# Layer 1's last two heads attended tile by tile in turns, with their projections placed ahead of them and the output weights loaded earlier

## Chip, cores and metric

The kernel runs on one NeuronCore of one Trainium2 chip. The metric is the device time of one execution in microseconds; for the kernel before it is the median of three runs.

## What is computed

The reference is a two-layer transformer block over 512 latent tokens and 256 context tokens of width 1024, batch 1, all in fp32. Each layer normalises its input and applies a shift and a scale from a conditioning vector, mixes the tokens by attention, adds the gated result, and adds a gated SwiGLU feed-forward part. The change touches layer 1 (the odd one) and the seam to its feed-forward part:

```python
def _diff_attend(q, k, v, lam):
    scale = HEAD_DIM ** -0.5
    def one_block(qb):
        s = jnp.einsum('bqhad,bkhad->bhaqk', qb, k).astype(jnp.float32) * scale
        p = jax.nn.softmax(s, axis=-1)
        a = (p[:, :, 0] - lam * p[:, :, 1]).astype(v.dtype)
        return jnp.einsum('bhqk,bkhe->bqhe', a, v)
...
def finish(o):
    o = _rms(o, subln_w) * (1.0 - lam_init)
    return o.reshape(o.shape[0], o.shape[1], -1) @ w_out
...
x = x + gx1 * ax
x = x + gx2 * _swiglu(_rms(x, norm_ffn_w[l]) * (1.0 + scx2) + shx2, ffn_w_in[l], ffn_w_out[l])
```

Layer 1 has 8 heads. Each head has two score matrices per query token over all 768 tokens (latent and context), and its output is the first softmax less lambda times the second, times the values. In the last layer only the 512 latent tokens are queries.

## The kernel before

All matrices are fp32. For the large products each operand is split into a high part (fp32r, names ending in h or hi) and the rest (names ending in l or lo), and three matmuls per block stand for one product. Tokens are worked on in tiles of 128: tiles 0 to 3 are latent, 4 and 5 context. The kernel is written in Tile: the program order of each engine's queue is dealt by a list scheduler (L1135) from the order of the Python code, priorities and buffers; each engine then works through its own queue in order.

Layer 1's mixer has three strands.

- **Projection.** `in_proj1` (L582) loads and splits a head's weights (SP loads wir, ACT casts wih, POOL or DVE subtracts wil), then for each of six token tiles sums q, k and v (names inps, 24 matmuls of 384 columns for latent tiles, 256 for context tiles, L411 to L413), copies the sum out of PSUM (qkv, ACT, L619), rotates and normalises it (qy on DVE and POOL, L622), splits it (qd and kd, on ACT, DVE L628 and POOL L631), and transposes it two tiles later (qpt L640 to qt L642, kpt L646 to kT L647). The generator `stream` (L1028) yields after each tile; `emit(n)` runs it until n of the 48 tiles are issued.
- **Attention.** One step is one head h and one query tile t, written (h, t). `attend1` computes the scores sc (L662, L663: two halves of four matmuls), their maxima mx (DVE, L665), the exponentials e (ACT, L667), and the difference (DVE, L674); after its yield come the transposes ppt (L681), their copies PT (DVE L684, ACT L686), the product av (L689), and the scaling and norm of the head's output o (L691 to L696). `Staggered.push` (L857) issues a step's first half, then the second half of the step before.
- **Way out.** `out_units` (L699) loads the eight weight rows wo (raw tiles wor, ACT cast woh, subtraction wol on POOL and DVE in turns, L316). `OutProj.operand` transposes a tile's eight head outputs (opt, L726 to L728) and `sums` makes two sums of 24 matmuls (ops, L736 to L738), to which `residual` (L418, L419) applies the gate g and adds x. `norm_hT` then norms the tile for the feed-forward part (square L282, scaling L284, transposes npt L289, hT L295 to L300), and `ffn` (L742) starts with gate and up products (pg, pu, L769) over two segments of 256 tokens, tiles 0 and 1, then tiles 2 and 3.

The loop at L1047 goes over heads, and inside over tiles. Each step is followed by `emit((h + 1) * NT + 2 + (2, 3, 5, 6)[t])`, one or two projection tiles. All 48 are issued by step (6, 2). At (7, 0) the projection's pools close, the weights of way out are asked for, into two shared raw buffers and one of their own, and at (7, 1) to (7, 3) operand and sums of the tile before are issued, the sums at low priority. After the loop come tile 3's operand and sums, four norms and the feed-forward part.

Of the kernel before, what the change touches and what calls it, by code (L numbers as in the profile page):

```python
# [10 lines left out]
F32 = mybir.dt.float32  # L11
F32R = mybir.dt.float32r
# [4 lines left out]
AP = bass.AP  # L17
# [46 lines left out]
def backbone(es: ExitStack, tc: tile.TileContext, x, c, ctx, c_ctx, mod_w, mod_b, norm_mix_w, norm_ffn_w,  # L64
# [179 lines left out]
    def gate_row(l, part, i, pool):  # L244

        if (l, part, i) not in gmem:
            gate_mem(l, part, i)
        g = pool.tile([P, D], F32, name=f"g{i}", tag=f"g{i}")
# [333 lines left out]
    def in_proj1(h, tabs, wp, st, wh, qp, late):  # L582
# [26 lines left out]
        for t in CTX_FIRST:  # L609
# [9 lines left out]
            nc.scalar.copy(raw[:, :n], ps)  # L619
# [15 lines left out]
            def transposes(t=t, nq=nq, qd=qd if nq else None, kd=kd):  # L635
                if nq:
                    pt = tr_tile("qpt", [P, 2, 2, P], F32R)
                    for j in range(2):
                        for a in range(2):
                            nc.tensor.transpose(pt[:, j, a, :], qd[:, j, a].rearrange("p a d -> p (a d)"), identr)  # L640
                    qt = qp.tile([P, 2, 2, P], F32R, name="qt", tag="qt", bufs=5)
                    nc.scalar.copy(qt, f32(pt))  # L642
# [10 lines left out]
    def attend1(h, t, state, o_t, nlam, subln, mp):  # L653
# [53 lines left out]
    class OutProj:  # L707
# [21 lines left out]

        def sums(self, t, bank=None, pool=None, add=nc.vector):  # L730
            ohi, olo = tile_T(0, t), tile_T(1, t)
            for n in range(2):
                ps = acc_tile("ops", one=bank)
                for k in range(KT):
# [3 lines left out]
                    nc.tensor.matmul(ps, olo[:, k, :], a, start=False, stop=k == KT - 1)  # L738
                residual(self.xs[t], ps, self.g[0 if t < NTX else 1], n, pool, add, 1)

# [305 lines left out]
    xs = [None] * NTX  # L1046
    for h in range(8):  # L1047
        for t in range(NTX):
            att.push(attend1(h, t, state[h], o_t, nlam, subln, at.pool))
            if h == 7 and t == 0:  # L1050
                wt.close()
                whi.close()
                wp.close()
                wlo.close()
                states[2].close()
                states[1].close()
                wp = Pool("w1", "right")
                opa = Pool("opa")
# [81 lines left out]
```

## Time and profile before

| | |
|---|---|
| median of 3 runs | 1811.46 us (1810.96 to 1811.88) |
| the profiled execution | 1812.21 us |
| its span, first to last instruction | 1810.4 us |
| mean granted TensorE clock | 0.990 |
| TensorE busy | 1737.3 us, 96% |
| layer 1's projections and attention | about 1030 to 1335 us of the span |
| from the last projection to the feed-forward part | about 1335 to 1424 us |

PE is TensorE's matmuls, PEld its weight loads, DVE VectorE, ACT ScalarE, POOL GpSimd, SP the engine that issues the transfers. In a wait row stand the waiting engine, its output and line, what it waited for, then the total, the number and the longest of the waits. In a row of the timeline stand the start in us from the span's begin, the duration, the engine, the line, the operation, output and inputs, the shape, and in brackets the idle time ahead with its releaser. A matmul's duration includes its way through the array, so that consecutive matmuls overlap: the rate is read from the starts.

### The profile page before, as it was taken

The page shows a single profiled execution, that of the slowest core. Times are in us where ns is not written, and L with a number is a line of the kernel's source. Part 1 is how long each engine was busy: PE and PEld are TensorE (multiplying, and loading weights), DVE is VectorE, ACT ScalarE, POOL GpSimd, SP SyncE. Part 2 cuts the span into 40 slices and gives each one's busy share as a digit, 9 for nine tenths or more (in the row PEclk, how much of TensorE's full clock was granted, in tenths as well). Part 3 has the DMA queues.
Part 4 walks back from the last instruction along what each step waited for, and adds up shares of the span by engine and source line. Part 5 has one row for each costly group of instructions (what it writes and reads, how often), then busy time and mean ns, then how long its engine had stood idle before and what let it go on. Part 6 is the DMA issues. An engine that isn't in the chain of part 4 may idle for free. (4 is left out here: it accounts for less than half of the span.)

```text
span 1810.4 us, 26150 instructions
## 1 busy us (share of the span) xinstructions
PE 1737.3 (96%) x9958; PEld 1456.4 (80%) x9958; DVE 1005.2 (56%) x1703; ACT 823.3 (45%) x1726; POOL 646.9 (36%) x840
## 2 busy tenths in 40 slices
PE   6999999999999999999999989999998999999998
PEld 4887776677888888888888788999986888888886
DVE  4766555444265555555543566666674455655652
ACT  6556556544354444343332656666564532221220
POOL 2864545532064344232210485667633200000000
PEclk9999999999999999999999999999999999999999
DMA  9112222313443234334320321111102332232321
GB/s 322 43 43 86 91 94 82 105 36 121 147 152 117 93 102 143 117 117 140 117 85 1 103 59 54 36 45 45 33 35 93 105 94 93 93 104 83 93 93 47
DMA packets 152477, 165.64 MB, mean 91 GB/s; under 512 B 16480, under 2 KB 139936, under 8 KB 152352
## 3 DMA queue, kind: packets, MB, share of 16 engines
q1 hardware_dynamic: 152000, 163.77, 28.2%
q8 instruction: 78, 1.28, 0.3%
q14 instruction: 47, 0.39, 0.1%
q10 hardware_dynamic: 352, 0.21, 0.0%
HBM read 159.73 MB, written 4.22 MB: 91 GB/s over the span
## 5 line engine op out<-in xcount | busy, mean ns | idle before, releaser
L769 PE MATMUL pg<-hT,wgh 128*128 128x512 f32 (+1 forms) x736 | 244.5, 386 | 3.9 <-ACT hT L299 3.7
L769 PE MATMUL pu<-hT,wuh 128*128 128x512 f32 (+1 forms) x736 | 243.2, 384 | 0.0
L418 DVE TENSOR_TENSOR dps<-dps,g 128x512 f32<-128x512 f32 x200 | 136.0, 697 | 135.0 <-PE dps L823 131.3
L821 PE MATMUL dps<-wdh,hdh 128*128 128x512 f32 x440 | 176.5, 402 | 5.6 <-DVE x L419 3.5
L822 PE MATMUL dps<-wdl,hdh 128*128 128x512 f32 x440 | 174.0, 396 | 0.0
L823 PE MATMUL dps<-wdh,hdl 128*128 128x512 f32 x440 | 166.6, 396 | 0.0
L769 PEld LDWEIGHTS pg<-hT,wgh 128*128 128x128 f32 x736 | 137.0, 189 | 34.4 <-ACT hT L299 3.9
L769 PEld LDWEIGHTS pu<-hT,wuh 128*128 128x128 f32 x736 | 136.6, 189 | 28.6
L769 PE MATMUL pg<-hT,wgl 128*128 128x512 f32 (+1 forms) x368 | 142.0, 386 | 0.0
L769 PE MATMUL pu<-hT,wul 128*128 128x512 f32 (+1 forms) x368 | 141.4, 384 | 0.0
L419 DVE TENSOR_TENSOR x<-x,dps 128x512 f32<-128x512 f32 x200 | 133.5, 684 | 3.4
L411 PE MATMUL inps<-wih,hT 128*128 128x384 f32 x384 | 133.4, 348 | 1.2 <-ACT qkv L619 0.5
L413 PE MATMUL inps<-wih,hT 128*128 128x384 f32 x384 | 131.2, 342 | 0.0
L412 PE MATMUL inps<-wil,hT 128*128 128x384 f32 x384 | 130.8, 341 | 0.0
L197 ACT ACTIVATE modw<-modw,cols 128x256 f32<-128x256 f32 x192 | 82.3, 498 | 69.2 <-DMA modw<-in_mod_w_dram 62.4
L821 PEld LDWEIGHTS dps<-wdh,hdh 128*128 128x128 f32 x440 | 82.7, 188 | 27.9 <-DVE x L419 4.4
L316 DVE TENSOR_TENSOR wul<-wur,wuh 128x1024 fp32r<-128x1024 f32 x44 | 54.9, 1247 | 88.0 <-ACT wuh L315 87.8
L769 PE MATMUL pg<-hTc,wgh 128*128 128x256 f32 x352 | 99.8, 287 | 3.9 <-ACT hTc L299 3.9
L769 PE MATMUL pu<-hTc,wuh 128*128 128x256 f32 x352 | 99.5, 286 | 0.0
L823 PEld LDWEIGHTS dps<-wdh,hdl 128*128 128x128 f32 x440 | 82.7, 188 | 20.2 <-issue 0.4
L796 DVE TENSOR_TENSOR pu<-sg,pu 128x768 f32<-128x768 f32 (+1 forms) x44 | 36.5, 829 | 111.2 <-PE pu L769 97.4
L822 PEld LDWEIGHTS dps<-wdl,hdh 128*128 128x128 f32 x440 | 82.8, 188 | 17.5
(235 smaller groups left out, 4290.6 us busy)
## 6 DMA issues: line engine op xcount, KB each, us to landing
modw<-in_mod_w_dram SPq DMA_DIRECT2D x96, 512.0 KB, 3.9
wgr<-in_ffn_w_in_dram SPq DMA_DIRECT2D x44, 512.0 KB, 3.4
wur<-in_ffn_w_in_dram SPq DMA_DIRECT2D x44, 512.0 KB, 3.4
wdr<-in_ffn_w_out_dram SPq DMA_DIRECT2D x44, 512.0 KB, 3.5
wir<-in_od_w_in_dram SPq DMA_DIRECT2D x96, 128.0 KB, 2.3
x<-in_x_dram SPq DMA_DIRECT2D x8, 512.0 KB, 3.7
wir<-in_ev_w_in_dram SPq DMA_DIRECT2D x16, 256.0 KB, 2.8
wor<-in_ev_w_out_dram SPq DMA_DIRECT2D x8, 512.0 KB, 3.5
```

The lines of the kernel that those rows point to most:

```text
L197: nc.scalar.activation(pr[:, k], w[:, k], AF.Copy, scale=cols[:, kk:kk + 1])
L316: (sub or nc.vector).tensor_sub(lo, raw, f32(hi))
L411: nc.tensor.matmul(ps, hs[0][:, k, :], a, start=k == 0, stop=False)
L412: nc.tensor.matmul(ps, hs[0][:, k, :], b, start=False, stop=False)
L413: nc.tensor.matmul(ps, hs[1][:, k, :], a, start=False, stop=k == KT - 1)
L418: nc.vector.tensor_mul(tmp, ps, g[:, n * 512:(n + 1) * 512])
L419: eng.tensor_add(xt[:, n * 512:(n + 1) * 512], xt[:, n * 512:(n + 1) * 512], tmp)
L769: nc.tensor.matmul(ps[:, s0:s1], a, cols_T(b, s0, s1)[:, k, :], start=k == 0 and q == 0, stop=k == KT - 1 and q == 2)
L796: nc.vector.tensor_mul(pu, sg, pu)
L821: nc.tensor.matmul(ps, hh, a, start=j == 0, stop=False)
L822: nc.tensor.matmul(ps, hh, b, start=False, stop=False)
L823: nc.tensor.matmul(ps, hl, a, start=False, stop=j == nj - 1)
```

## The change

The loop now goes over a list of 32 steps: heads 0 to 5 as before, each over its four tiles, then for each tile head 6 and head 7 in turn: (6, 0), (7, 0), (6, 1), (7, 1) and so on. While i is under 24 each step emits up to `10 + 38 * i // 23` projection tiles, so that all 48 are issued by the end of head 5. At i = 24, ahead of the last eight steps, the projection's pools close and way out's weights are asked for, into the two shared raw buffers alone. The gate row and the residual's scratch get a place in the buffer that context tokens had (`ctx_room`), and the two norm rows another; operand and sums of a tile follow after head 7 of the next tile has begun, and the norms of tiles 0 and 1 are now issued inside the loop, at t = 2 and 3, where head 7 stands. Four buffer counts differ: qkv 4 to 3, qt 5 to 8, o1 2 to 1, and `residual` gets its scratch tiles from outside.

```diff
-            raw = wp.tile([P, 384], F32, name="qkv", tag="qkv", bufs=4)
+            raw = wp.tile([P, 384], F32, name="qkv", tag="qkv", bufs=3)
...
-                    qt = qp.tile([P, 2, 2, P], F32R, name="qt", tag="qt", bufs=5)
+                    qt = qp.tile([P, 2, 2, P], F32R, name="qt", tag="qt", bufs=8)
...
-        o1 = mp.tile([P, P], F32, name="o1", tag="o1", bufs=2)
+        o1 = mp.tile([P, P], F32, name="o1", tag="o1", bufs=1)
...
-    def residual(xt, ps, g, n, pool=None, eng=nc.vector, rb=2):
+    def residual(xt, ps, g, n, tmps=None, eng=nc.vector):
 
-        tmp = ps if pool is None else pool.tile([P, 512], F32, name="rtmp", tag="rtmp", bufs=rb)
+        tmp = ps if tmps is None else tmps[n]
...
-    for h in range(8):
-        for t in range(NTX):
-            att.push(attend1(h, t, state[h], o_t, nlam, subln, at.pool))
-            if h == 7 and t == 0:
...
-                ws = out_units(wp.pool, od_w_out, (nc.gpsimd, nc.vector), (raw_tile, raw_tile, lambda shape, name:
-                               opa.pool.tile(shape, F32, name=name, tag="wor", bufs=1)))
-                oproj = OutProj(1, ws, o_t, xs, opa.pool)
-            if h == 7 and 0 < t <= 3:
-                oproj.operand(t - 1)
-
-                with tc.high_priority(-1000):
-                    oproj.sums(t - 1, 0, opa.pool, nc.gpsimd)
-            emit((h + 1) * NT + 2 + (2, 3, 5, 6)[t])
+    steps = [(h, t) for h in range(6) for t in range(NTX)] + [(h, t) for t in range(NTX) for h in (6, 7)]
+    for i, (h, t) in enumerate(steps):
+        att.push(attend1(h, t, state[h], o_t, nlam, subln, at.pool))
+        if i < 24:
+            emit(10 + 38 * i // 23)
+        if i == 24:
+            for pool in (wt, whi, wp, wlo, states[2]):
+                pool.close()
+            wp = Pool("w1", "right")
+            ws = out_units(wp.pool, od_w_out, (nc.gpsimd, nc.vector))
+            misc, room = ctx_room([P, 2, KT, P], F32, "room")
+            misc = misc.rearrange("p a k q -> p a (k q)")
+            room = [room[:, j] for j in range(2)]
+            oproj = OutProj(1, ws, o_t, xs, misc[:, 0])
+            tmp = [misc[:, 1, 512 * n:512 * (n + 1)] for n in range(2)]
+        if i > 26 and h == 7:
+            oproj.operand(t - 1)
+
+            with tc.high_priority(-1000):
+                oproj.sums(t - 1, 0, tmp, nc.gpsimd)
+            if t > 1:
+                norm_hT(t - 2, xs[t - 2], 1, 1, None, room=room)
     att.flush()
-    for t in range(3, NTX):
-        oproj.operand(t)
-        oproj.sums(t)
-    room = ctx_room([P, 2, KT, P], F32, "nroom")
-    for t in range(NTX):
-        norm_hT(t, xs[t], 1, 1, None, room=[z[:, t % 2] for z in room])
-    opa.close()
+    oproj.operand(3)
+    oproj.sums(3)
+    for t in range(2, NTX):
+        norm_hT(t, xs[t], 1, 1, None, room=room)
+    states[1].close()
```

The scheduler deals the queues anew. The first place is PE's queue at the start of layer 1, where head 0's first latent tiles are transposed (qpt, kpt). Before, the rows that end the projection of a latent tile (its last two are the first two rows here, of 24) stand right ahead of them:

```order
L412 MATMUL inps<-wil,hT_110 128x384
L413 MATMUL inps<-wih,hT_111 128x384
L640 MATMUL qpt<-identr,qd 128x128 x4
L646 MATMUL kpt<-identr,kd 128x128 x2
L640 MATMUL qpt<-identr,qd 128x128 x2
L662 MATMUL sc<-kT,qt 128x256
L663 MATMUL sc<-kT,qt 128x256
L662 MATMUL sc<-kT,qt 128x256
L663 MATMUL sc<-kT,qt 128x256
L640 MATMUL qpt<-identr,qd 128x128 x2
L646 MATMUL kpt<-identr,kd 128x128 x2
```

After, the two last rows of the second context tile's projection (256 columns) stand ahead of them:

```order
L412 MATMUL inps<-wil,hTc_4638 128x256
L413 MATMUL inps<-wih,hTc_4639 128x256
L640 MATMUL qpt<-identr,qd 128x128 x4
L662 MATMUL sc<-kT,qt 128x256
L663 MATMUL sc<-kT,qt 128x256
L662 MATMUL sc<-kT,qt 128x256
L663 MATMUL sc<-kT,qt 128x256
L646 MATMUL kpt<-identr,kd 128x128 x2
L640 MATMUL qpt<-identr,qd 128x128 x4
L646 MATMUL kpt<-identr,kd 128x128 x2
L411 MATMUL inps<-wih,hT_110 128x384
```

The 24 rows of that latent tile's projection have moved behind the transposes of two tiles and the first four scores. On ACT the copy L619 of the second context tile has moved behind both tiles' casts.

The second place is PE's queue at the last projection of all. Before:

```order
L411 MATMUL inps<-wih,hT_110 128x384
L412 MATMUL inps<-wil,hT_110 128x384
L413 MATMUL inps<-wih,hT_111 128x384
L662 MATMUL sc<-kT,qt 128x512
L663 MATMUL sc<-kT,qt 128x512
L662 MATMUL sc<-kT,qt 128x256
L663 MATMUL sc<-kT,qt 128x256
L662 MATMUL sc<-kT,qt 128x512
L663 MATMUL sc<-kT,qt 128x512
L689 MATMUL av<-vv,PT 128x128 x4
L640 MATMUL qpt<-identr,qd 128x128 x4
```

After:

```order
L411 MATMUL inps<-wih,hT_110 128x384
L412 MATMUL inps<-wil,hT_110 128x384
L413 MATMUL inps<-wih,hT_111 128x384
L640 MATMUL qpt<-identr,qd 128x128 x4
L646 MATMUL kpt<-identr,kd 128x128 x2
L662 MATMUL sc<-kT,qt 128x256
L663 MATMUL sc<-kT,qt 128x256
L662 MATMUL sc<-kT,qt 128x256
L663 MATMUL sc<-kT,qt 128x256
L640 MATMUL qpt<-identr,qd 128x128 x4
L646 MATMUL kpt<-identr,kd 128x128 x2
```

Counted over the whole queue, 218 score matmuls of layer 1 (27.25 steps of eight) and 150 products av stand ahead of the last projection matmul before, 200 (25 steps) and 138 after. Behind it, 34 scores stand ahead of the first out-projection matmul before and 36 after. On PE, 91 matmuls of the feed-forward part's first segment stand between tile 3's last ops and its norm's transposes npt before, 67 after. After, the first ops come behind all eight opt of tile 0; before, behind seven.

The third place is SP's and ACT's queue at way out and at the last norm. SP before:

```order
L311 DMA wor<-in_od_w_out_dram 128x1024 x8
L250 DMA g_14081<-gmem 128x1024
L322 DMA x_14377<-out_dram 128x1024
L311 DMA wgr<-in_ffn_w_in_dram 128x4x256 x2
L322 DMA x_14476<-out_dram 128x1024
L311 DMA wur<-in_ffn_w_in_dram 128x4x256 x2
L311 DMA wdr<-in_ffn_w_out_dram 128x1024 x2
```

SP after (the first x is that of tile 2):

```order
L311 DMA wor<-in_od_w_out_dram 128x1024 x6
L322 DMA x_14398<-out_dram 128x1024
L311 DMA wor<-in_od_w_out_dram 128x1024 x2
L250 DMA room_13877<-gmem 128x1024
L311 DMA wgr<-in_ffn_w_in_dram 128x4x256 x2
L322 DMA x_14523<-out_dram 128x1024
L311 DMA wur<-in_ffn_w_in_dram 128x4x256 x2
```

The load of x for tile 2, into the place that o of tile 0 leaves, now stands ahead of the last two rows of way out's weights. ACT before, around the square (L282) and the scaling (L284) of tile 3, x_14476:

```order
L295 ACTIVATE nroom_14547<-npt,modc_107,aff_109 128x128 x4
L282 ACTIVATE nroom_14546,nss<-x_14476 128x1024
L299 CAST hT_110<-nroom_14547 128x4x128
L315 CAST wdh<-wdr 128x1024
L284 ACTIVATE nroom_14546<-x_14476,rs_n 128x1024
L315 CAST wdh<-wdr 128x1024
L315 CAST wgh<-wgr 128x1024
L295 ACTIVATE nroom_14547<-npt,modc_107,aff_109 128x128 x4
```

ACT after, with tile 3 as x_14523:

```order
L295 ACTIVATE room_13878<-npt,modc_107,aff_109 128x128 x4
L299 CAST hT_110<-room_13878 128x4x128
L315 CAST wdh<-wdr 128x1024 x2
L282 ACTIVATE room_13878,nss<-x_14523 128x1024
L315 CAST wgh<-wgr 128x1024
L284 ACTIVATE room_13878<-x_14523,rs_n 128x1024
L315 CAST wgh<-wgr 128x1024
L295 ACTIVATE room_13878<-npt,modc_107,aff_109 128x128 x4
```

Both casts of wd now stand ahead of tile 3's square; before, one stood ahead of the scaling and one behind it.

More of the change, by code (lines that the diff above doesn't have):

```diff
@@ L247, in gate_row @@
             gate_mem(l, part, i)
-        g = pool.tile([P, D], F32, name=f"g{i}", tag=f"g{i}")
+        g = pool if isinstance(pool, AP) else pool.tile([P, D], F32, name=f"g{i}", tag=f"g{i}")
         with tc.issue_after(turn["load"].ins):
@@ L728, in operand, with sums @@
                 nc.vector.tensor_sub(olo[:, 4 * q:4 * q + 4], pt, f32(ohi[:, 4 * q:4 * q + 4]))
-        def sums(self, t, bank=None, pool=None, add=nc.vector):
+        def sums(self, t, bank=None, tmps=None, add=nc.vector):
             ohi, olo = tile_T(0, t), tile_T(1, t)
@@ L738, in sums @@
                     nc.tensor.matmul(ps, olo[:, k, :], a, start=False, stop=k == KT - 1)
-                residual(self.xs[t], ps, self.g[0 if t < NTX else 1], n, pool, add, 1)
+                residual(self.xs[t], ps, self.g[0 if t < NTX else 1], n, tmps, add)
     def ffn(l, xs, ntok, wp, fp, done, mods=()):
@@ L1046, in backbone @@
     xs = [None] * NTX
-    for h in range(8):
-        for t in range(NTX):
-            att.push(attend1(h, t, state[h], o_t, nlam, subln, at.pool))
-            if h == 7 and t == 0:
[L1051 to L1058, printed above, removed]
-                ws = out_units(wp.pool, od_w_out, (nc.gpsimd, nc.vector), (raw_tile, raw_tile, lambda shape, name:
-                               opa.pool.tile(shape, F32, name=name, tag="wor", bufs=1)))
-                oproj = OutProj(1, ws, o_t, xs, opa.pool)
-            if h == 7 and 0 < t <= 3:
-                oproj.operand(t - 1)
-                with tc.high_priority(-1000):
-                    oproj.sums(t - 1, 0, opa.pool, nc.gpsimd)
-            emit((h + 1) * NT + 2 + (2, 3, 5, 6)[t])
```

## Prediction

> **What bounds the kernel now.** The head of the page comes first, with the totals by engine.
>
> ```profile
> span 1810.4 us, 26150 instructions
> PE 1737.3 (96%) x9958; PEld 1456.4 (80%) x9958; DVE 1005.2 (56%) x1703; ACT 823.3 (45%) x1726; POOL 646.9 (36%) x840
> ```
>
> TensorE (PE) works 96% of the span, and the change takes no matmul away. Time can come or go only as idle time or slow clock of PE, so each part below is counted in lost PE time. The windows from layer 1's first projections to its output projection show where it is lost: behind the two times stand the busy us of PE, PEld, DVE, ACT, POOL, then the granted clock.
>
> ```profile
> 1040.00:1060.00 20.00, 17.42 (x119) 16.66 (x118) 8.43 (x17) 9.65 (x24) 18.33 (x26) 1.00 0.28 79
> ...
> 1080.00:1100.00 20.00, 16.85 (x125) 15.62 (x126) 16.80 (x28) 14.14 (x37) 15.14 (x24) 1.00 0.39 113
> ...
> 1120.00:1140.00 20.00, 16.97 (x117) 15.38 (x116) 17.48 (x27) 12.69 (x33) 15.26 (x21) 0.94 0.29 80
> ...
> 1160.00:1335.00 175.00, 171.90 (x1185) 164.03 (x1184) 122.35 (x228) 110.78 (x290) 113.04 (x178) 0.99 0.13 36
> 1335.00:1345.00 10.00, 7.74 (x46) 6.24 (x46) 6.02 (x12) 7.94 (x19) 4.25 (x8) 0.86 0.00 0
> 1345.00:1365.00 20.00, 15.35 (x99) 12.60 (x98) 19.75 (x27) 15.81 (x35) 9.77 (x9) 0.98 0.30 106
> 1365.00:1375.00 10.00, 8.71 (x38) 6.85 (x39) 6.32 (x8) 4.05 (x7) 2.84 (x2) 0.66 0.74 263
> ```
>
> The projection stage is nearly dense (171.90 of 175 us), with losses of about 3 us in three windows early on. The loss comes after it: from 1335 to 1365 PE is busy 23.09 of 30 us while VectorE (DVE) is at 19.75 of 20. PE's waits from 1334 to 1460 name the stalls (total, times, longest).
>
> ```profile
> PE pg L769 <- ACT hT L299: 3.7, 1, 3.7
> PE ops L737 <- DVE wol L316: 3.1, 1, 3.1
> PE sc L662 <- ACT e L667: 1.6, 3, 0.8
> ...
> PE ppt L681 <- DVE hT L728: 1.2, 1, 1.2
> ...
> PE kpt L646 <- POOL kd L631: 0.8, 1, 0.8
> ```
>
> 3.7 us are lost before the feed-forward part's second segment (tile 3's norm), 3.1 us on a way out's weight that DVE had not split, 1.2 us on a transposed attention output right after.
>
> Slow clock comes on top. PE's rows show it (start, us), from the first score behind the last projection at 1334.82 to the first out-projection matmuls at 1357.45 and those 15 us later:
>
> ```profile
> 1334.82 0.40 PE L662 MATMUL sc<-kT,qt 128*128 128x512 f32 x1
> 1335.06 0.40 PE L663 MATMUL sc<-kT,qt 128*128 128x512 f32 x1
> 1335.29 0.28 PE L662 MATMUL sc<-kT,qt 128*128 128x256 f32 x1
> 1335.41 0.28 PE L663 MATMUL sc<-kT,qt 128*128 128x256 f32 x1
> ...
> 1335.99 1.05 PE L689 MATMUL av<-vv,PT 128*128 128x128 f32 x8
> 1336.80 0.54 PE L640 MATMUL qpt<-identr,qd 128*128 128x128 f32 x4
> ...
> 1343.73 0.63 PE L663 MATMUL sc<-kT,qt 128*128 128x512 f32 x1
> 1344.15 0.63 PE L662 MATMUL sc<-kT,qt 128*128 128x512 f32 x1
> ...
> 1357.45 0.48 PE L736 MATMUL ops<-woh,hT 128*128 128x512 f32 x1
> ...
> 1371.98 0.63 PE L736 MATMUL ops<-woh,hT 128*128 128x512 f32 x1
> 1372.41 0.63 PE L737 MATMUL ops<-wol,hT 128*128 128x512 f32 x1
> ```
>
> A 512-column matmul starts 0.42 us after the one before in the slow spells (1343.73 to 1344.15, 1371.98 to 1372.41), and 0.24 otherwise (1334.82 to 1335.06); 256 columns take 0.12 (1335.29 to 1335.41). The spell around 1343 to 1346 costs about 1.4 us, half its length, the one from 1366 to 1373 about 3.3, half of some 6.6 us of work: 4.7 together.
>
> **The change, part by part.**
>
> *Moved work, cost zero by itself.* The order puts 25 steps' scores ahead of the last projection, where 27.25 stood before. So 18 score matmuls, 12 transposes and 12 products with V move behind it. At the warm pitches that is nine scores each of 0.24 and 0.12 us (3.2), 24 passes of products (two per matmul in the trace) at 0.10 (eight from 1335.99 to 1336.80: 2.4), and 12 transposes at the same 0.10 with their share of gaps (1.4): 7.0 us of PE work. The last projection ends 7.0 us earlier if the stage before loses the same, and the same work is done later. What matters is what is lost in it.
>
> *Behind the last projection: -4.0 us.* First what goes. Way out's weights are asked for at step 24 instead of step 28, and DVE and GpSimd (POOL) split them while PE still has attention. I cost the 3.1 us stall, the 1.2 us on L728 and the slow spell of 3.3 us behind them at nothing: -7.6. What hides the splits is attention of tiles 1 and 2: four splits each on POOL and DVE take 10.2 and 8.3 us (the last two rows below), against some 20 us from the loads to the first sums; if that cover failed the 3.1 would be back. Then what comes. A step without a projection beside it is bound by DVE:
>
> ```profile
> L665 DVE TENSOR_REDUCE mx<-sc 128x1 f32<-128x768 f32 x48 | 45.0, 950 | 12.5 <-PE sc L663 12.4
> ...
> L674 DVE SCALAR_TENSOR_TENSOR e<-e,rt 128x768 f32<-128x768 f32 x24 | 34.9, 1456 | 0.7
> ...
> L684 DVE COPY PT<-ppt 128x256 f32<-128x256 f32 x25 | 10.4, 416 | 1.8 <-PE ppt L681 1.6
> ...
> L316 POOL TENSOR_TENSOR wol<-wor,woh 128x1024 fp32r<-128x1024 f32 x4 | 10.2, 2551 | 8.4 <-ACT woh L315 8.4
> ...
> L316 DVE TENSOR_TENSOR wol<-wor,woh 128x1024 fp32r<-128x1024 f32 x4 | 8.3, 2079 | 0.3 <-ACT woh L315 0.3
> ```
>
> Two maxima (1.90), L674 (1.46), a copy (0.42) and some 0.6 of small ones make 4.4 us of DVE per step; PE needs about 3.3 (scores 0.7, transposes 0.6, products 1.3, query and key transposes 0.55, and gaps). 2.25 more such steps lose 2.25 x 1.1, about +2.4. The first out-projection matmul now stands behind all eight transposes of tile 0, the last of which waits for DVE to finish head 7: I take +1.2, about one row that can stand ahead of it on DVE (0.95 to 1.46), bounds 0 and 2.4. The last two loads of weights stand on SP behind the load of x for tile 2, because there are two raw buffers instead of three; the second half of the first sum starts after them in my walk, still covered by attention of tile 1, bounds 0 to +3, taken 0. Last, the norm wait:
>
> ```profile
> 1434.78 1.06 ACT L315 CAST wdh<-wdr 128x1024 fp32r<-128x1024 f32 x1 [1.49 <-DMA wdr<-in_ffn_w_out_dram]
> ...
> 1437.01 1.36 DVE L297 TENSOR_SCALAR nroom<-npt,aff,modc 128x128 f32<-128x128 f32 x4
> ...
> 1438.42 1.50 ACT L295 ACTIVATE nroom<-npt,modc,aff 128x128 f32<-128x128 f32 x4
> ...
> 1440.47 0.39 PE L769 MATMUL pg<-hT,wgh 128*128 128x256 f32 x1 [3.70 <-ACT hT L299]
> ```
>
> Before, 91 matmuls of the first feed-forward segment stand between tile 3's last sum and the norm's transposes; after, 67 (some 8 us at 0.12). That cover shrinks by 24 x 0.12 = 2.9 us. Against it, tile 2's norm no longer stands in front of tile 3's on both engines: its L295 and L297, of the size of the rows above, are 1.50 + 1.36 = 2.9 us. In the new order both wd casts (ACT) and the wd splits (DVE) stand ahead of tile 3's square and of its last addition, so the load of wdr, for which ACT waited 1.49 us here, comes onto the chain; with fewer norms in the queue it is asked for as early relative to it, and I take 0, bounds -2.9 and +2.9. Sum: -7.6 + 2.4 + 1.2 = -4.0. Bounds: -8 (no price for DVE's steps) to +3 (the weights late again, and the norm wait longer by its whole lost cover).
>
> *Slow clock in the longer stretch: +2.0.* The walk is at full clock. The spells in before cost 4.7 up to 1440; a stretch with more gaps could have them too. Nothing in before shows it, so bounds 0 and +4.7; I take 2.0, the nearer row being 1335 to 1345 (clock 0.86), not 1365 to 1375. The Trainium skill's page "TensorE: Matmul & The Clock Gate", section "Part 1: The HAM clock gate", says that the clock is halved after an idle window of about 3.4 us and comes back after as long a busy one. The halving agrees with the trace (0.42 against 0.24 us), but the drop near 1341 came in a stretch whose single gaps were at most 0.8 us (the kpt row of the waits). By the rule taken strictly no gap of my walk is long enough, this term would be 0 and the time 1809.
>
> *Layer 1's start: +3.4 us.* In the new order PE goes from the second context projection straight into the query transposes; before, one more projection of 24 matmuls stood between. The rows of before (start, us):
>
> ```profile
> 1053.25 0.28 PE L413 MATMUL inps<-wih,hTc 128*128 128x256 f32 x1
> ...
> 1054.05 0.45 PE L411 MATMUL inps<-wih,hT 128*128 128x384 f32 x1 [0.52 <-ACT qkv L619]
> ...
> 1055.83 0.43 DVE L628 TENSOR_TENSOR qd<-qy,qd 128x256 fp32r<-128x256 f32 x1 [4.96 <-ACT qd L627]
> ...
> 1057.50 0.61 POOL L622 TENSOR_TENSOR qy<-qy,rs_q 128x256 f32<-128x256 f32 x1
> ...
> 1058.33 0.45 PE L640 MATMUL qpt<-identr,qd 128*128 128x128 f32 x4
> ...
> 1060.50 0.41 PE L411 MATMUL inps<-wih,hT 128*128 128x384 f32 x1
> ```
>
> Tile 0's qd is ready at 1055.83 + 0.43 = 1056.26, when PE has stood since 1053.53: 2.7 us. Then tile 1's rows come no sooner than POOL's L622 at 1057.5 allows: I walk tile 1's transposes to 1059.6, and the context tile's copy (L619), moved behind them on ACT, sets the next projection at about 1059.6. It begins 0.9 us sooner than before's at 1060.50, but with one projection less done (24 matmuls from 1054.05 to 1058.33, 4.3 us): 4.3 - 0.9 = 3.4. Bounds 0 (PE's delay lets DVE and ACT run ahead, and later waits shrink by as much) to +5 (the three qkv buffers make the copy wait longer).
>
> *The rest of the projection stage: -1.5 us.* 38 tiles go over 23 steps, 1.65 a step instead of 1.5, so attention is about 6% thinner per us of PE. The three early windows lose 2.6, 3.2 and 3.0 us, with DVE at 84 and 87% in two of them. Taking a quarter of those two (6.2) as gone is -1.5; bounds -4 and +3, since every engine's rows are dealt anew and a scheduler's order can put a maximum behind a split again. The buffers qt 8, o1 1 and the shared scratch tiles add no instruction: 0.
>
> **Sum.** -4.0 + 2.0 + 3.4 - 1.5 = -0.1. The profiled execution takes 1812.2 us (span 1810.4 and 1.8 outside), 0.75 above the median of 1811.46. So 1812.1 for such an execution and **1811 us** for the median.
>
> **Rivals.**
>
> *The start's stall is made up and no slow spell comes: faster.* For it: after such a stall DVE and ACT have work in hand, and the next windows have waits to give up. Against: the stage from 1160 is dense and has only 3.1 us to give. Price: -4.0 - 1.5, and as much again from waits that shrink, with the two other terms at 0, about 1804.
>
> *PE runs at half clock in the stretch without projections: slower.* Place: from the last projection to the first out-projection matmul, 22.6 us before (1334.8 to 1357.4), about 29.6 after by my walk, with some 19 us of work. At the clock 0.66 of 1365 to 1375 this takes 28.8 us, and DVE, which waits for each score in turn, is late by most of the 9.8 more. With 2 us already in the sum, +8 is left: 1819. It decides if PE does under about half its time's work over some 4 us there, as at 1338 to 1342. For it: 7.3 steps in a row with DVE as bound. Against: two steps in flight give PE something to do in most gaps.
>
> *The change hardly does what it says.* The last heads' projections were already ahead of most of their attention, the order moves only 2.25 steps' scores, and PE's total is fixed: all terms near zero, 1811.5. For it: PE's busy share of 96%. Against: the rows that wait in the two stretches are rows that the order moves.
>
> **How the numbers follow.** Forecast (1807 to 1816 by its own bounds) 0.46, faster rival 0.22, slower rival 0.24, no effect 0.08. A measurement of this kernel tells about 0.2% from no change, 3.6 us: 1807.8 and 1815.1. Of the forecast's chance 0.30 lies within, 0.08 below, 0.08 above. Faster 0.22 + 0.08 = 0.30; within 0.30 + 0.08 = 0.38; slower 0.24 + 0.08 = 0.32. The range for 8 in 10 reaches to both rivals with their neighbourhood: 1801 to 1821.
>
> **What would show it.** Right: a wait of the query transposes for qd of 2 to 3 us at about 1054; no wait on wol over 1 us; the last projection ending near 1330 (1334.8 - 7.0 + 3.4 - 1.5); a wait of the second segment on L299 of 3 to 4 us. Wrong: windows behind the last projection with a clock under 0.8 over 20 us (slower rival); the stage's early windows above 18 of 20 (faster rival); first out-projection matmuls waiting for the last wo loads, behind x for tile 2.

## The result, and the profile after

The changed kernel takes 1822.45 us (median of six, 1818.94 to 1827.48) against 1812.01 for the kernel before in the same rounds: ratio 1.0054, 95% interval [1.0041, 1.0066]. Measured again on another occasion the ratio was 1.0068 [1.0054, 1.0081]. It is slower by 10 to 12 us, 1.4 us outside the stated range.

The windows of the changed kernel, cut at about the same places of the program as those of before (behind the two times the busy us of PE, PEld, DVE, ACT, POOL, then the granted clock):

```profile
1040.00:1060.00 20.00, 15.11 (x101) 13.98 (x100) 8.64 (x17) 9.37 (x24) 18.25 (x26) 0.92 0.28 79
1060.00:1080.00 20.00, 19.33 (x109) 18.17 (x108) 11.45 (x25) 10.38 (x31) 11.78 (x24) 0.91 0.00 1
1080.00:1100.00 20.00, 18.03 (x131) 16.73 (x130) 17.70 (x29) 15.51 (x38) 15.54 (x18) 1.00 0.33 84
1120.00:1140.00 20.00, 19.15 (x137) 18.08 (x136) 16.25 (x28) 14.21 (x37) 13.04 (x16) 1.00 0.15 44
...
1330.00:1340.00 10.00, 6.53 (x37) 5.38 (x36) 4.07 (x9) 4.87 (x14) 3.28 (x6) 0.83 0.01 2
1340.00:1370.00 30.00, 27.13 (x181) 22.71 (x180) 28.56 (x41) 25.39 (x55) 14.90 (x14) 1.00 0.46 151
1370.00:1380.00 10.00, 7.15 (x28) 5.53 (x28) 7.26 (x14) 3.62 (x10) 2.64 (x3) 0.83 0.42 126
1380.00:1430.00 50.00, 47.32 (x259) 38.74 (x258) 17.15 (x33) 21.52 (x42) 13.43 (x19) 1.00 0.07 22
```

The start has lost more PE time (15.11 of 20 us, before 17.42), the two windows after it less (18.03 and 19.15 against 16.85 and 16.97). Behind the last projection the thin place has moved: 1340 to 1370 is denser than before's 1345 to 1365, and a new hole stands at 1370 to 1380, in which DVE too works only 7.26 of 10 us. PE's waits behind 1330:

```profile
PE ops L736 <- DVE room L418: 4.3, 3, 2.9
PE pg L769 <- ACT hT L299: 3.0, 1, 3.0
PE qpt L640 <- ACT qd L627: 3.0, 1, 3.0
PE dps L821 <- ACT hdh L424: 1.5, 1, 1.5
```

The 3.1 us on wol are gone, as the prediction had it; the wait on L728 is 0.8 instead of 1.2. In their place stands a wait of a sum (ops) for the residual's first multiplication (L418), 2.9 us at its longest. Right behind the last projection the query transposes now wait 3.0 us for qd (0.6 before).

Since runs differ by some us ahead of layer 1, the profiles are aligned at a small matmul just ahead of it (lps, L574) that no run changes. From there, in us, to the last projection matmul, the first out-projection matmul, the feed-forward part's second segment, and the span's end:

| | last projection | first ops | second segment | end |
|---|---|---|---|---|
| before | 300.3 | 323.1 | 406.1 | 776.0 |
| after | 295.4 | 321.8 | 412.0 | 782.6 |
| after, again (e9) | 295.9 | 322.9 | 413.2 | 784.0 |

The projections end 4.9 us sooner. Behind them has moved the work that the prediction priced at 7.0 us; PE's rows in the two traces show 18 transposes ppt moved (156 to 138 stand ahead) where the prediction counted 12, so by its pitches it is 7.7 us, and 2.8 us are lost up to there. The first sums begin 1.3 us sooner. By the second segment the kernel is 5.9 us late, of the 6.6 us at the end.

From the first ops to the second segment it takes 7.2 us longer than before. Most of that is moved work: PE's rows there hold 20 scores, 30 ppt and 60 passes of av instead of 4, 18 and 36, some 6.7 us by the prediction's pitches. The windows from the last projection to the first ops and from there to the second segment, of before and then of the changed kernel:

```profile
1334.65:1357.45 22.80, 19.29 (x127) 16.31 (x127) 18.41 (x31) 17.39 (x43) 7.51 (x12) 0.93 0.19 70
1357.45:1440.47 83.02, 73.53 (x406) 61.41 (x404) 42.07 (x63) 41.50 (x74) 26.12 (x28) 0.96 0.29 96
1329.90:1356.32 26.42, 20.86 (x136) 17.33 (x135) 19.18 (x33) 19.70 (x48) 12.10 (x16) 0.94 0.18 62
1356.32:1446.50 90.18, 80.30 (x456) 66.86 (x456) 48.33 (x77) 47.71 (x89) 24.96 (x31) 0.98 0.31 95
```

Among the sums PE is idle 9.9 us, before 9.5: what the change took away there has come back as something else. The two profiled executions of the changed kernel were the fastest of their rounds, 1818.94 and 1819.56 us; the other 4 us of the medians' difference is in no profile.

### The profile page after: what moved, and what is told of

It is laid out like the page before. It is cut to its first block, busy times and chain, and to the rows that moved or that the text cites. A ratio compares the mean times of both kernels' runs of the same rounds, so it can differ in the third digit from the quotient of the medians.

```text
span 1817.1 us, 26168 instructions
## 1 busy us (share of the span) xinstructions
PE 1735.2 (95%) x9958; PEld 1452.0 (80%) x9958; DVE 999.7 (55%) x1703; ACT 823.4 (45%) x1726; POOL 645.5 (36%) x840
## 5 line engine op out<-in xcount | busy, mean ns | idle before, releaser
L418 DVE TENSOR_TENSOR dps<-dps,g 128x512 f32<-128x512 f32 x200 | 136.0, 697 | 138.3 <-PE dps L823 133.3
```

## Experiments

Ratios are against the kernel before in the same rounds, with the 95% interval; "aligned end" is the last column of the table above. Where two runs are compared, their ratios are. The aligned figures scatter from run to run: in the eight traces whose rows are the same up to the last projection matmul (after, e3, e4, e6, e9, e11, e12, r18) it stands at 293.0 to 296.1 us, and in the three with before's rows (before, e7, r16) at 296.1 to 300.3. A difference of 2 or 3 us between two aligned figures can be chance.

### The start: e1 and e2

e1 is the kernel before with one number changed.

```diff
-            raw = wp.tile([P, 384], F32, name="qkv", tag="qkv", bufs=4)
+            raw = wp.tile([P, 384], F32, name="qkv", tag="qkv", bufs=3)
```

> The kernel before with only the number of qkv buffers lowered from 4 to 3. Theory (the start's stall is lasting and comes from this count alone): PE's queue at layer 1's start is the one of the changed kernel, the query transposes wait 1 to 3 us near 1054, the clock drops for about 5 us, and the run is 3.5 to 6 us slower than before. Rival (the projection stage makes it up): the same waits near 1054, but the last projection ends within 1.5 us of before's and the time is within 2 us of it.

Measured: 1.0022 [1.0011, 1.0032], some 4 us. PE's queue at layer 1's start is that of the changed kernel row for row, so this buffer count alone makes it. The window there:

```profile
1050.00:1060.00 10.00, 6.94 (x52) 6.25 (x52) 4.24 (x8) 3.42 (x9) 9.49 (x12) 1.00 0.30 83
1060.00:1070.00 10.00, 9.35 (x43) 8.63 (x44) 4.83 (x11) 4.84 (x16) 7.38 (x16) 0.66 0.00 0
```

After the thin stretch the clock is at 0.66 for 10 us and PE does 43 instructions where before did 66. The last projection ends at 302.5, 2.2 us later than before's, the latest of the three with its rows. So the stall lasts in part: the stage makes up more than half of stall and slow clock. The rest of e1's loss in the profile (aligned end 783.1, of an execution 4 us above e1's median) lies behind the projections, where its queues differ too.

e2 is the changed kernel with `bufs=4` for qkv and `bufs=7` for qt.

> The changed kernel with 4 qkv buffers as before, and 7 qt buffers instead of 8, which makes the room for it. Theory (start's stall lasting, and about half of the loss): 4 to 6 us faster than the changed kernel, some 4 to 6 us slower than before; the last projection ends near 1326. Rival (the loss is all behind the last projection): within 2 us of the changed kernel, 8 to 10 slower than before.

Measured: 1.0041 [1.0026, 1.0056]; last projection at 293.5, 1.9 us sooner than after's, aligned end 778.6. Neither in full: the greater part of the loss stays. The five traces with these buffers (e2, e5, e10, r13, r14) have the last projection at 293.5 to 297.1, at 294.1 in the middle, against 295.4 for the eight of the changed kernel's kind. So the start is worth 1 to 2 us, which is within the scatter.

### Behind the last projection: e3, e4, e6

e3 gives way out's weights a third raw buffer:

```diff
-            ws = out_units(wp.pool, od_w_out, (nc.gpsimd, nc.vector))
...
+            ws = out_units(wp.pool, od_w_out, (nc.gpsimd, nc.vector),
+                           (raw_tile, raw_tile, lambda shape, name: misc[:, 1]))
```

> The changed kernel with a third raw buffer for way out's weights (the scratch of the residual, free until then). Theory (the first sums are late because the last two weight rows are loaded late and split late): the last wol ends 5 us or more sooner, the wait on L418 near 1374 shrinks from 2.9 to under 1 us, and the run is 3 to 5 us faster than the changed kernel. Rival (the stretch is bound by DVE's attention, whatever the weights do): the wait moves to another row, within 1.5 us of the changed kernel.

Measured: 1.0034 [1.0022, 1.0046], aligned end 779.9. The longest wait on L418 is 0.9 us, and the last split of a weight ends 8.0 us sooner. The theory holds in kind and is at the lower end in size (2.7 us by the profile): late weights are a part, not the whole.

e4 lets the sums of tiles 0 to 2 use both banks:

```diff
-                oproj.sums(t - 1, 0, tmp, nc.gpsimd)
+                oproj.sums(t - 1, None, tmp, nc.gpsimd)
```

> The changed kernel with the sums of tiles 0 to 2 taking turns between both PSUM banks instead of using one. Theory (PE waits because the next sum needs the bank that L418 has still to read, while L418 stands behind attention's rows on DVE): no wait of a sum on L418 over 0.6 us, 3 to 5 us faster than the changed kernel. Rival (the other bank is attention's, so av waits for the sums in its place): waits of av on the bank of 2 us or more, and within 1.5 us of the changed kernel or slower.

Measured: 0.9992 [0.9982, 1.0001], aligned end 775.0: level with before. The gain is twice what the theory gave. Its waits behind 1040 show the rival's price as well:

```profile
PE sc L662 <- ACT e L667: 5.5, 10, 1.0
...
PE av L689 <- DVE room L418: 2.2, 1, 2.2
```

A product av now waits 2.2 us for the bank, and no sum waits for L418 any more.

e6 takes the low priority from the sums (`with tc.high_priority(-1000)` left out).

> The changed kernel with the in-loop sums at normal instead of low priority, still in one bank. Theory (the loss is the bank that L418 has to free): sums come a little sooner, but L418 still stands behind attention's rows on DVE, and the time is within 2 us of the changed kernel. Rival (the loss is the sums' low priority, which puts them and L418 late in the queues): 4 us or more faster than the changed kernel, with no wait of a sum on L418 over 1 us.

Measured: 1.0044 [1.0032, 1.0056], aligned end 782.5, waits on L418 4.2 us in all, 2.8 the longest. PE's rows have the same clump as the changed kernel's (shown with e12). The sums' low priority is not the cause.

### Which part of the change makes the hole: e8, e11, e12

e8 puts the last eight steps back in the old order:

```diff
-    steps = [(h, t) for h in range(6) for t in range(NTX)] + [(h, t) for t in range(NTX) for h in (6, 7)]
+    steps = [(h, t) for h in range(8) for t in range(NTX)]
...
-        if i > 26 and h == 7:
+        if h == 7 and t:
```

> The changed kernel with the last eight steps in the old order, head 6 over its tiles and then head 7, so that the sums of tile 0 come after step (7, 1) as before; pace, early weights, buffers and norms as changed. Theory (the tile order puts the first sums among seven steps of attention, where DVE is late with L418): the waits on L418 fall under 1 us and the run is 3 us or more faster than the changed kernel, though the start's 2 us stay. Rival (the earlier end of the projections alone makes the stretch DVE-bound): within 1.5 us of the changed kernel.

Measured: 1.0064 [1.0051, 1.0078], aligned end 787.3. The theory falls: the wait on L418 is down to 0.7 us, but sums wait 5.8 us for L727 instead, 4.8 the longest. The tile order is not what costs.

e11 asks for the weights at step 27 (`if i == 27:`).

> The changed kernel with the pools closed and way out's weights asked for at step 27 instead of 24. Theory (the early start of the weights is worth the splits' stall that it took away): the first sum waits 3 us or more for wol, 3 to 6 us slower than the changed kernel. Rival (the loads and splits are paced by raw buffers and by attention's rows on ACT and DVE, not by the step at which they are asked for): within 1.5 us of the changed kernel.

Measured: 1.0070 [1.0058, 1.0082] beside 1.0068 for e9 in the same call, aligned end 782.8. The time is the rival's, but the run tests neither: in its trace the rows of PE, DVE, ACT and POOL from layer 1 on are those of the changed kernel, one for one, so the scheduler dealt the same queues. It serves as one more repeat of the changed kernel. What an early start of the weights is worth stays open.

e12 moves the norms of tiles 0 and 1 behind the loop again:

```diff
-            if t > 1:
-                norm_hT(t - 2, xs[t - 2], 1, 1, None, room=room)
     att.flush()
     oproj.operand(3)
     oproj.sums(3)
-    for t in range(2, NTX):
+    for t in range(NTX):
         norm_hT(t, xs[t], 1, 1, None, room=room)
```

> The changed kernel with the norms of tiles 0 and 1 after the loop instead of inside it. Theory (they take no place that anybody waits for): within 1.5 us of the changed kernel, the wait on L299 ahead of the second segment 3 to 4 us in both. Rival (done early, they shorten the queue ahead of tile 3's norm): the wait on L299 grows by 2 us or more, and so does the time.

Measured: 1.0006 [0.9995, 1.0016] beside 1.0068 for e9 in the same call: 0.6% or 11 us, the whole loss. Neither the theory nor the rival had it so: the wait on L299 is 2.6 us, less than with the norms inside. The queue says why. In the changed kernel PE's rows behind the last transpose of tile 1 are 48 matmuls of sums, eight norm transposes and 24 more matmuls of sums, and only then the rows ppt and av of the last three steps. With the norms after the loop, ppt and av of the same steps stand among the sums. Up to this place PE's rows from layer 1 on are the same in both traces. On the chip, PE of the changed kernel at the hole:

```profile
1371.11 0.39 PE L738 MATMUL ops<-woh,hT 128*128 128x512 f32 x1
1371.34 0.30 PE L726 MATMUL opt<-cst,o 128*128 128x128 f32 x1
1374.49 0.79 PE L736 MATMUL ops<-woh,hT 128*128 128x512 f32 x1 [2.85 <-DVE room L418]
1375.09 0.63 PE L737 MATMUL ops<-wol,hT 128*128 128x512 f32 x1
1375.51 0.63 PE L738 MATMUL ops<-woh,hT 128*128 128x512 f32 x1
```

DVE of the changed kernel in the same us:

```profile
1371.83 0.21 DVE L673 SCALAR_TENSOR_TENSOR rt<-sm,nlam,rc 128x1 f32<-128x1 f32 x1
1371.96 0.95 DVE L665 TENSOR_REDUCE mx<-sc 128x1 f32<-128x768 f32 x1
1372.83 1.01 DVE L674 SCALAR_TENSOR_TENSOR e<-e,rt 128x768 f32<-128x768 f32 x1
1373.76 0.69 DVE L418 TENSOR_TENSOR room<-ops,room 128x512 f32<-128x512 f32 x1
```

PE ends the first sum at 1371.5 and stands at the next sum, whose bank L418 has still to read; L418 waits its turn on DVE behind a maximum and L674 and runs at 1373.76. The matmuls behind the wait start 0.42 us apart, the slow clock. PE of e12 at the same place:

```profile
1375.62 0.39 PE L738 MATMUL ops<-woh,hT 128*128 128x512 f32 x1
1375.84 0.30 PE L726 MATMUL opt<-cst,o 128*128 128x128 f32 x1
1376.47 0.66 PE L681 MATMUL ppt<-cst,e 128*128 128x128 f32 x4 [0.33 <-DVE hT L728]
1378.23 1.16 PE L689 MATMUL av<-vv,PT 128*128 128x128 f32 x8 [1.10 <-ACT PT L686]
1379.22 0.60 PE L681 MATMUL ppt<-cst,e 128*128 128x128 f32 x4
1379.58 0.48 PE L736 MATMUL ops<-woh,hT 128*128 128x512 f32 x1
1379.89 0.39 PE L737 MATMUL ops<-wol,hT 128*128 128x512 f32 x1
1380.12 0.40 PE L738 MATMUL ops<-woh,hT 128*128 128x512 f32 x1
```

DVE of e12 there:

```profile
1376.46 0.95 DVE L665 TENSOR_REDUCE mx<-sc 128x1 f32<-128x768 f32 x1
1377.33 1.01 DVE L674 SCALAR_TENSOR_TENSOR e<-e,rt 128x768 f32<-128x768 f32 x1
1378.26 0.68 DVE L418 TENSOR_TENSOR room<-ops,room 128x512 f32<-128x512 f32 x1
```

DVE is no faster: L418 starts 2.6 us after the start of the sum's last matmul in both. But PE works on attention meanwhile, waits 1.4 us instead of 2.85, and the clock stays full: from 1379.89 to 1380.12 a sum's matmul starts 0.23 us after the one before. And later, where the changed kernel does the rest of attention by itself, e12 is dense. Its windows:

```profile
1374.00:1384.00 10.00, 8.57 (x50) 7.01 (x49) 7.76 (x14) 5.19 (x13) 3.88 (x5) 1.00 0.42 131
1384.00:1394.00 10.00, 10.00 (x62) 8.70 (x60) 2.94 (x6) 5.22 (x12) 3.51 (x7) 1.00 0.01 2
1394.00:1434.00 40.00, 40.00 (x224) 34.14 (x223) 17.83 (x32) 18.88 (x36) 12.23 (x15) 1.00 0.12 36
```

40.00 of 40 us, where the changed kernel has 47.32 of 50 in 1380 to 1430. The whole stretch from the first ops to the second segment, with the same work as the changed kernel's 90.18 us:

```profile
1360.85:1442.53 81.68, 76.83 (x455) 65.90 (x455) 46.13 (x75) 44.39 (x87) 26.50 (x30) 1.00 0.28 90
```

It is 8.5 us shorter, with 4.9 us of idle PE time instead of 9.9 and no slow clock. Aligned, e12's second segment starts at 404.0, 8 us sooner, and the end is at 773.4.

### The control: e9

No edit; the changed kernel beside e10 to e12 on the same chip.

> The changed kernel as it is, beside the runs below on the same chip. If its loss is 6 to 7 us as the profiles aligned at layer 1's first small matmul say, the ratio is 1.0025 to 1.0045; if it is 10 us as its first six times say, 1.0045 to 1.0065.

Measured: 1.0068 [1.0054, 1.0081], above both brackets. The profiles' 6.6 to 8.0 us are short of it by some 4 us, as said above.

### Do the mends add up: e5, e10, r13, r14, r18

e5 joins e2 and e4.

> The changed kernel with 4 qkv buffers (7 qt) and with the sums taking turns between both banks. Theory (the start's stall and the one bank are separate losses): the gains add, 2 us at the last projection and 4 to 6 us behind it, so that the span from layer 1's first rows to the end is 8 to 10 us shorter than the changed kernel's, and the time 1 to 4 us below before's. Rival (both feed the same slack): no faster than with two banks alone, within 1 us of before.

Measured: 1.0009 [0.9999, 1.0020]. The profile is 9.8 us shorter than after's (aligned end 772.8), as the theory says, but the timed runs are no faster than e4's 0.9992. The rival holds by the times.

e10 adds e3's raw buffer to e5.

> The changed kernel with 4 qkv buffers, two banks and the third raw buffer. Theory (the weights come later than PE could use them): another 1 to 3 us behind the last projection than with the first two alone, 0.1 to 0.3% faster than before. Rival (with two banks the late weights are covered by the other bank's sum): within 1 us of the first two alone.

Measured: 1.0020 [1.0008, 1.0031], aligned end 775.4. No gain; the rival holds. In these runs late weights cost only while the sums have one bank (e3).

r13 is e12 with e2's buffers.

> The changed kernel with the norms of tiles 0 and 1 after the loop and 4 qkv buffers (7 qt). Theory (two separate losses, start and norms): 1 to 2 us faster than with the norms after the loop alone, its stretch from layer 1's first small matmul to the end about 771 to 772 us, 0 to 0.2% faster than before. Rival (the start's 2 us are slack once the tail is mended): the same as with the norms after the loop alone.

Measured: 1.0001 [0.9991, 1.0010], aligned end 771.4. The profile has the 2 us, within its scatter; the ratio, 0.0005 under e12's, can't tell them from nothing.

r14 is r13 with both banks.

> As the run with norms after the loop and 4 qkv buffers, with the sums taking turns between both banks as well. Theory (one bank and the norms' place are one loss, a clump of sums in PE's queue without attention beside it): no faster than that run, within 1.5 us. Rival (two losses): another 3 us or more.

Measured: 1.0021 [1.0008, 1.0033], aligned end 779.0. No gain, rather 0.2% worse.

r18 is e12 with both banks, buffers as changed.

> The changed kernel with the norms of tiles 0 and 1 after the loop and the sums taking turns between both banks, all else as changed. Theory (one loss): within 1.5 us of the run with the norms after the loop alone. Rival (two losses): 3 us or more faster than it, and then faster than before.

Measured: 1.0023 [1.0013, 1.0034], aligned end 777.7, again 0.17% above e12. One bank and the norms' place are one loss: whichever of the two is mended takes it away, and both together do not gain more. In r14 and r18 the feed-forward part's first segment waits 4.1 us on L299.

### The same parts in the kernel before: e7, r15, r16, r17

e7 gives before's sums both banks (`oproj.sums(t - 1, None, opa.pool, nc.gpsimd)`).

> The kernel before with its in-loop sums taking turns between both banks. Theory (in before the sums follow each other with little of attention left on DVE, so one bank costs only the 1.1 us of waits on L418): within 1.5 us of before. Rival (one bank costs before as much): 4 us or more faster than before.

Measured: 1.0013 [1.0002, 1.0024], aligned end 776.8. A little slower, no gain: before has no such hole.

r15 is e12 with e8's order of steps, heads in order.

> The changed kernel with the norms after the loop and the last eight steps in the old order, head 6 and then head 7. Theory (the tile order itself gains by bringing sums beside attention): 3 to 6 us slower than with the norms after the loop alone. Rival (the order of the steps is worth nothing): within 1.5 us of it.

Measured: 1.0061 [1.0049, 1.0074] against e12's 1.0006, some 10 us; aligned end 785.8. The theory holds and is topped: once the norms are out of the loop, the tile order is worth 0.55%. Without it a sum waits 5.1 us for L727. Beside e8 (1.0064) it also shows that with the heads in order the norms' place hardly matters here: inside the loop the norms cost what the tile order gains.

r16 is before with the norms of tiles 0 and 1 inside its loop.

```diff
                     oproj.sums(t - 1, 0, opa.pool, nc.gpsimd)
+                if t > 1:
+                    norm_hT(t - 2, xs[t - 2], 1, 1, None, room=[z[:, t % 2] for z in room])
```

> The kernel before with only the norms of tiles 0 and 1 moved into its loop, behind the sums at (7, 2) and (7, 3). Theory (norms at normal priority pull the low sums they need forward, ahead of attention's tail, in any order of steps): PE's queue has 72 out-projection matmuls in a row ahead of the tail of attention, and the run is 4 us or more slower than before. Rival (only together with the tile order): within 2 us of before.

Measured: 1.0025 [1.0013, 1.0037], 4.5 us, with 72 matmuls of sums in PE's queue, broken only by operand and norm transposes, and attention's tail behind them. The theory holds: the norms' place clumps the sums in the old order too. The aligned end (775.1) hides the cost, because the stage ahead, with the rows of before, ended 4.2 us sooner in this run. From the last projection to the second segment it takes 109.1 us, before 105.8: 3.3 us.

r17 is before with the new pace.

```diff
-            emit((h + 1) * NT + 2 + (2, 3, 5, 6)[t])
+            emit(min(48, 10 + 38 * (4 * h + t) // 23))
```

> The kernel before with only the pace of the projections as changed (all 48 tiles by step 24), order of steps, weights, buffers and norms as before. Theory (the last eight steps of attention then stand alone, bound by DVE, and way out's sums come only behind them): 5 us or more slower than before, the loss between the last projection and the first out-projection matmul. Rival (the scheduler spreads attention anyway): within 2 us of before.

Measured: 1.0059 [1.0040, 1.0078], 11 us, aligned end 783.0. Its windows around the last projection, which ends at 1339.6:

```profile
1320.00:1340.00 20.00, 20.00 (x133) 19.50 (x132) 14.55 (x30) 11.59 (x32) 10.04 (x18) 1.00 0.00 1
1340.00:1360.00 20.00, 14.81 (x92) 12.74 (x91) 11.85 (x21) 12.98 (x32) 7.39 (x10) 0.83 0.06 17
1360.00:1380.00 20.00, 16.60 (x109) 14.79 (x108) 19.06 (x30) 14.36 (x34) 9.03 (x12) 0.90 0.35 120
1380.00:1400.00 20.00, 18.14 (x86) 14.55 (x85) 7.02 (x10) 6.55 (x12) 6.40 (x7) 0.84 0.46 154
```

The theory holds in size, in place only in part. From the last projection to the first sum it takes 30.6 us (329.8 less 299.2 aligned) instead of 22.8, with PE at 14.81 of the first 20 us and a clock of 0.83. But this stretch holds 40 scores, 36 ppt and 72 passes of av, before 34, 18 and 48; by the prediction's pitches that is 5.6 us of moved work, so some 2 us are lost here. Nearly 4 us are lost ahead of the last projection, which ends 1.1 us sooner with some 4.9 us less work; before's rows alone scatter by as much there.

### The sum of the parts

The early end of the projections costs 0.6% by itself (r17); that this is so because attention then stands alone is shown only in part. The tile order pays it back (e12 against r15, 0.55%), for it brings the first sums beside attention. The norms inside the loop take that away again (e9 against e12, 0.6%), for they put the sums in a clump. What is left is the difference measured. The start's stall is 1 to 2 us in the profiles, within their scatter, and in the changed kernel hardly seen in the ratios (r13 against e12). None of these versions is clearly faster than before; e4 (0.9992) and r13 (1.0001) are level with it.

## Why the prediction was wrong

- **The moved work and the last projection: right.** Forecast to end near 1330; it ended at 1330.2 (295.4 aligned, 4.9 sooner). The start (+3.4) and the rest of the stage (-1.5) together were to lose 1.9; measured 2.8, with 18 moved transposes instead of the 12 of the prediction's count. That the end fits so closely is in part luck: runs with the same rows differ by 3 us there.
- **The start: right in mechanism, with the cause narrowed.** The query transposes waited 1.5 us for qd, less than the 2 to 3 forecast, and a score then 0.7 for qt; a projection ahead of them waited 1.8 for the copy L619, before 1.0. The clock was 0.66 from 1055 to 1065. I put the walk's stall at 3.4 and left the clock there out; at the last projection 1 to 2 us of both are left (e1, e2). The cause is one buffer count (e1).
- **The weights' stall: right.** No wait on wol over 1 us. Whether asking for the weights earlier did that is open, since step 27 in place of 24 left the queues the same (e11).
- **Behind the last projection, "-4.0", bounds -8 to +3, and slow clock "+2.0": wrong.** This is the step that failed. Together they were -2.0. Measured, from the last projection to the second segment: 116.6 against 105.8 us, less 7.7 of moved work, +3.1. Up to the first ops it is 3.6 us longer with about 1.2 us more work: 2.4 lost, no more than the sum had there (2.4 for DVE-bound steps and 1.2 for the eight transposes), though by a wait that it didn't name, 2.98 us of the query transposes for qd. From the first ops on the sum had -7.6, for waits and a slow spell that were to cost nothing behind attention. Measured there +0.5 (7.2 longer, 6.7 more work). In e12, the same work with the norms behind the loop, that stretch gives -8.0. So the old losses did go as forecast, and the norms in the loop, whose place the sum put at nothing there, brought 8.5 us in their stead. The sum took attention as the cover of everything else: "still covered by attention of tile 1", bounds 0 to +3, taken 0, for the first sum. The order showed otherwise: behind tile 1's transposes stand 72 matmuls of sums, broken only by eight norm transposes, with the rest of attention behind them. At the first turn from one sum to the next the bank was not free, and nothing stood in PE's queue that could run (2.85 us and a slow spell); the rest of attention came alone later. The prediction looked at how far the norms shorten tile 3's queue (the wait on L299: 3 to 4 us forecast, 3.0 measured) and not at what they pull forward. The slow clock left in the sum up to the second segment (4.7 - 3.3 + 2.0 = 3.4 us) agrees with two spells of 0.83 over 10 us, but by luck: one of them stands at the hole that the sum did not have.
- **The rivals.** The slower one (half clock between the last projection and the first sum) gave about the time measured, but by another mechanism: that stretch was 26 us instead of the walk's 29.6, and the clock was low for a part of it only (0.83 from 1330 to 1340, 1.00 from 1340 to 1370). The rule that I had weighed (the Trainium skill, "TensorE: Matmul & The Clock Gate", "Part 1: The HAM clock gate": an idle window of about 3.4 us), by which this term would be 0, did not hold: the clock fell behind single waits of 2.98 and 2.85 us. The faster one's start made up its stall in part, as e1 shows.
- **Not settled.** Why the scheduler lets the norms draw the sums forward: low priority of the sums isn't it (e6). And the 4 us by which the timed executions of the changed kernel exceed its profiled ones.

## What to carry to other kernels

Before moving work, read in the program order what it pulls with it: here two norms that nobody waited for drew 72 matmuls ahead of the attention that was to cover their waits, and cost all that a better order of the steps had gained. An early end of one stage was a loss by itself here (r17), and was paid back only with work placed beside what remained. When two stretches are compared, count the work in each first: of the 7.2 us that the changed kernel takes longer among its sums, 6.7 are moved work. Where sums follow each other in one PSUM bank, ask which engine reads the bank and what stands ahead of it there; here a second bank and other work in between were the same remedy, and one was enough.

## What the runs showed of the hardware

The granted clock fell without any long idle time: in e1 it was 0.66 from 1060 to 1070, after a window in which PE was busy 6.94 of 10 us and its waits were at most 1.6 us. In the changed kernel it was 0.83 from 1330 to 1340 (one wait of 3.0) and from 1370 to 1380 (one of 2.85). A clock of 0.83 over 10 us is 1.7 us lost, so, as an estimate from these figures, a wait of 3 us in this kernel is worth nearer 5. How long the clock stays low differs from run to run: in e9, with the same rows, it was 0.69 from 1330 to 1340.
